# An eighth, half-deep set of block products for columns of the gate and the merge gate, an attention stage advanced at each half tile, and eleven warm-up matmuls

## The chip, the cores and the metric

The kernel runs on one core of one Trainium2 chip. The metric is the device time of one execution in microseconds (us), as the median of several runs.

Five engines work side by side and are tied by semaphores: TensorE (PE in the profile; its weight loads are listed apart as PEld), VectorE (DVE), ScalarE (ACT), GpSimd (POOL) and SyncE (SP). SP and POOL also hold the queues from which most DMA transfers are issued. Matmuls write their sums to PSUM, which the kernel uses as two rings of four banks, called `mm` and `bg`.

## What is computed

One decoder layer over 256 tokens and 2048 channels, in float32. A single input projection feeds two parallel token mixers and two merge gates:

```python
h = rmsnorm(x, pre_norm_g[l])
proj = h @ w_in[l]
(a_q, a_k, a_v, a_g, a_lr, b_q, b_k, b_v, b_g, m_a, m_b) = jnp.split(proj, offsets, axis=-1)
...
o_a = rmsnorm(o_a, gla_norm_g[l]).reshape(B, S, GLA_VAL_DIM) * jax.nn.silu(a_g)
y_a = o_a @ w_branch_a[l]
...
o_b = o_b.reshape(B, S, DIFF_VAL_DIM) * jax.nn.silu(b_g)
y_b = o_b @ w_branch_b[l]
merged = jax.nn.sigmoid(m_a) * y_a + jax.nn.sigmoid(m_b) * y_b
out = merged @ w_out[l]
x = x + rmsnorm(out, post_norm_g[l])
```

`o_a` is gated linear attention with 4 heads, `o_b` is differential attention with 16 heads. The change concerns 512 columns of `a_g` (the fourth group of the gate, "ag3" in the kernel) and 512 columns of `m_a` (the third group of the merge gate, "m02").

## The kernel before

**Three matmuls for one.** Each float32 operand is split into a part `hi` in a shorter format and the remainder `lo`. A product is the sum hi x hi, hi x lo and lo x hi. For the weights the split is made on the fly in half tiles of 128 x 1024: ACT writes `hi` (L345), DVE writes `lo` = raw - hi (L346). Both have rings of three buffers. `take` hands the next split half tile to the matmuls and emits the splits of up to three later half tiles (`AHEAD = 3`), in an order fixed beforehand in `seq`.

**Plain tiles.** `token_major` computes 512 columns for all 256 tokens over the full depth of 2048: eight half tiles, each of two depth blocks x two token halves x three matmuls = 12 matmuls of 512 columns. `channel_major` computes 128 channels with the channels on the partitions: two half tiles of 8 matmuls of 512 and 8 of 256 columns each.

**Sets of block products.** A set covers 1024 columns as two groups of 512, left and right, and forms the 2 x 2 block product (two token halves, two depth halves, two column groups) with seven products instead of eight, numbered 1 to 7 and run in the order `PRODUCTS = (1, 3, 5, 6, 2, 7, 4)`. The sums of token halves are made once, at the start. The sums of weight blocks are made while the set runs, in the tiles `a` and `b` of the tag `chain`, which has four slots: `link` loads a block, `follow_set` adds another block into it by a DMA with addition on POOL's queue (L240) or adds two tiles on DVE (L248), always after the split that reads the older value. Product 1 reads `a`; product 3 reads `b`; products 5, 6 and 4 read `a` after one more addition each; product 2 reads a third tile, `c`, that SP loads; product 7 reads `b` after one addition. There are seven sets, 0 to 6. Each product of a set has four half tiles (two quarters of the depth `t`, two halves `h` each) of 6 matmuls. The results of a set are combined in `block_products` and spilled to DRAM (`gspill`), from where later stages fetch them.

**The order of the phase.** `phase_steps` writes the order of the sets' half tiles by hand, with the half tiles of 88 other projections (`v4`, the keys and queries of both mixers) between them: one other half tile after each pair of half tiles of a set, two at the front, none at the places in `skip`. In this phase the matmuls are pinned to this order.

**After the phase** come ag0 to ag3 (the gate), m02, the heads of group 3 (eight channel projections dq30 to dk33), m03, then the branch projections y00 to y03, and a branch stage in which the half tiles of y03, y10 and y11 alternate with a smaller set `ys0`. Between their half tiles the attention runs as generators in a list `tasks`: `pump(n)` lets the first n tasks take one step each, after every second half tile of a plain tile and after each channel projection. `gla_scores` makes the scores of the linear attention in two halves, `gla_out` weighs the values (`weigh`, L513 in the profile) and transposes the result (`turn_heads`, L1016), and two lanes `diff_lane` run the pairs of heads of the differential attention. A task that yields "go" is called eager: `pump_eager` also lets it take a step after the half tiles in between. `settle` and the loop on `"out"` pump without matmuls of their own where a result is needed that is not there yet.

**The start.** `WARM` matmuls on ones run on TensorE before the first weights are split (L432). The first weights are those of v0, whose matmuls stand at L528.

Of the kernel before, what the change touches and what calls it, by code (L numbers as in the profile page):

```python
# [24 lines left out]
LANES = 3  # L25
X_LOADS = {0: (2, 2), 1: (4, 4), 2: (8, 4), 3: (12, 4)}
ROWS = {"two": 2, "tok": 4, "chan": KT}
WARM = 9
PRODUCTS = (1, 3, 5, 6, 2, 7, 4)
SETS = 7  # L30
MERGE = (0, 1, 6)
LEAD = 6
# [16 lines left out]
def chunk_plan():  # L49

    plan = [("v0", "two", "w_in", [(6144, RANK), (2048, 2 * VG[0] - RANK)])]
    at = 2 * VG[0] - RANK
    for g, n in enumerate(VG[2:]):
        plan.append((f"v{g + 2}", "tok", "w_in", [(2048 + at, n)]))
        at += n
    for hf in range(2):
        for name, base in (("k", 1024), ("q", 0)):
            for c in range(4):
                plan.append((f"{name}{hf}{c}", "chan", "w_in", [(base + 512 * hf + P * c, P)]))
    o = 6144 + RANK  # L60
    for s in range(2):
        plan.append((f"set{s}", "set", "w_in", [(o + 10240 + 1024 * s, 1024)]))
    for s in range(2, 6):
        plan.append((f"set{s}", "set", "w_in", [(o + base + 512 * (s - 2), 512) for base in (4096, 6144)]))
    plan.append(("set6", "set", "w_in", [(o + 8192, 1024)]))
    for g in range(4):
        plan.append((f"ag{g}", "tok", "w_in", [(4096 + 512 * g, 512)]))
        for c in range(4):
            for n, name in enumerate(("dq", "dk")):
                plan.append((f"{name}{g}{c}", "chan", "w_in", [(o + 2048 * n + 512 * g + P * c, P)]))  # L70
        if g > 1:
            plan.append((f"m0{g}", "tok", "w_in", [(o + 8192 + 512 * g, 512)]))
        for br in range(2):
            kind = "late" if br and g < 2 else "tok"
            plan.append((f"y{br}{g}", kind, ("w_branch_a", "w_branch_b")[br], [(512 * g, 512)]))
        plan.append((f"o{g}", "late", "w_out", [(512 * g, 512)]))
    plan.append(("ys0", "half", "w_branch_b", [(c, 512) for c in BRANCH_COLS]))
    for s, cols in enumerate(LATE_COLS):
        plan.append((f"os{s}", "half", "w_out", [(c, 512) for c in cols]))
    return plan  # L80


def tiles_of(n, kind):

    if kind == "set":
        return [(8 * i + 4 * t, 4, 512 * j, 512) for i in range(2) for j in range(2) for t in range(2)]
    if kind == "half":
        return [(4 * i, 4, 512 * j, 512) for i in range(2) for j in range(2)]
    if kind == "late":
        return [(r, 4, 0, n) for r in (8, 12)]  # L90
    return [(r, ROWS[kind], 0, n) for r in range(0, KT, ROWS[kind])]


def phase_steps():
# [4 lines left out]
    slots = [(s, prod, t) for s in range(SETS) for prod in PRODUCTS for t in range(2)]  # L99
    front = [(0, prod, t) for prod in PRODUCTS[:2] for t in range(2)]  # L100
    skip = [(SETS - 1, 4, 1)] + [(s, prod, 0) for prod in (4, 2, 1) for s in range(SETS - 1, 0, -1)]
# [35 lines left out]
def hybrid_kernel(ctx: ExitStack, tc, xt, xn, preg, postg, w, w2, gkb, glag, lamv, diffg, ident_d, causal_d, lmask_d, out):  # L137
# [75 lines left out]

    def link(s, name, t):
        count[0] += 1
        c = blocks.tile([P, 2048], F32, tag="chain", name=f"{name}_{count[0]}", bufs=4)
        (pool if s else sp).dma_start(c, weights(f"set{s}", {"a": 0, "b": 6}[name] + t)[0])
        chain[s, name, t] = c

    def emit_set(s, prod, t, h):  # L220
        c = slice(1024 * h, 1024 * h + 1024)
        if h == 0 and s + 1 < SETS and (prod, t) in ((7, 1), (4, 0)):
            link(s + 1, "a", 1 - t)
        if h == 0 and s + 1 < SETS and (prod, t) == (4, 1):
            link(s + 1, "b", 0)
        if h == 0 and prod == 1 and (s == 0 or t == 0):
            link(s, "b", t if s == 0 else 1)
        n = 4 * PRODUCTS.index(prod) + 2 * t + h + LEAD - 4 * PRODUCTS.index(2)
        if 0 <= n < 4:
            i, j = n // 2, n % 2  # L230
            raws[s, i, j] = u([P, 1024], "c")
            sp.dma_start(raws[s, i, j], weights(f"set{s}", 4 + i)[0][:, 1024 * j : 1024 * j + 1024])
# [3 lines left out]
    def follow_set(s, prod, t, h):  # L236
        c = slice(1024 * h, 1024 * h + 1024)

        def accumulate(name, i):
            pool.dma_start(chain[s, name, i][:, c], weights(f"set{s}", 2 + i)[0][:, c], accum_op=ALU.add)  # L240
# [3 lines left out]
        i = {(5, 1): 0, (6, 0): 1, (2, 1): 0, (7, 0): 1}.get((prod, t))  # L244
# [309 lines left out]
    def token_major(key, n, ops, step=1, upto=KT // 2):  # L554
        banks = [ps("mm"), ps("mm")]
        for q in range(upto):
            half_tile(banks, n, q, ops, *take(key))
# [188 lines left out]
    gspill = [None] * (2 * SETS)  # L746

    def merge_gate(banks):
        t = u2([P, 2, 512], "mgate")
        for b in range(2):  # L750
            act.activation(t[:, b, :], banks[b], AF.Tanh, scale=half_rstd[:, b : b + 1])
# [59 lines left out]
    def block_products(s):  # L811
# [4 lines left out]
        def right_done(b):  # L816
            dst = halves["r"][:, b, :]
            if s in MERGE:
# [6 lines left out]
        def left_done(b, src):  # L825
            if s in MERGE:
                act.activation(halves["l"][:, b, :], src, AF.Tanh, scale=half_rstd[:, b : b + 1])
            else:
                act.activation(halves["l"][:, b, :], src, AF.Copy, scale=rstd[:, b : b + 1])

        for prod in PRODUCTS:
# [3 lines left out]
            for t in range(2):  # L835
                for h in range(2):
                    hi, lo = take(("set", s, prod, t, h))
                    for w, parts in ((hi, (0, 1)), (lo, (0,))):
                        for j in range(2):
                            kt = 4 * t + 2 * h + j  # L840
                            a = operand(prod, kt)
                            for part in parts:
                                first = prod not in (6, 7, 4) and kt == 0 and w is hi and part == 0
                                last = kt == 7 and w is lo
                                i = mm(out, a[part], w[:, 512 * j : 512 * j + 512], start=first, stop=last, skip_group_check=out is x)
                    latest[0] = i.ins
                    if t and h:
# [25 lines left out]
    sets = (step for s in range(SETS) for step in block_products(s))  # L873
# [3 lines left out]
    for n, step in enumerate(phase_steps()):  # L877
        if n == PUT_OFF:
            put_off.pop()()
        if step == ("set", SETS - 1, 7, 1, 1):  # L880
# [103 lines left out]
    def gla_out():  # L984
# [44 lines left out]
        for n in range(6):  # L1029
# [6 lines left out]
            if n > 1:  # L1036
                for j in range(2):
                    turn_heads(n // 2 - 1, 2 * (n % 2) + j)
            yield
# [204 lines left out]

    for g in range(4):
        banks = token_major(f"ag{g}", 512, x_ops, LANES)
        t = u2([P, 2, 512], "ua")
        for b in range(2):
            gate(banks[b], b, t[:, b, :])
# [21 lines left out]
    merge_gate(token_major("m02", 512, x_ops, LANES))  # L1271
# [361 lines left out]
```

## Time and profile before

| What | Value |
|---|---|
| Median of 3 runs | 1090.25 us |
| Lowest and highest run | 1090.04 and 1090.7 us |
| The profiled execution | 1092.18 us |
| Its span in the trace | 1090.3 us |
| Instructions | 15340 |
| Phase of the sets, end | 590.65 us |
| ag0 to ag3, end | 689.2 us |
| m02, end | 717.6 us |
| Heads of group 3, end | 775.4 us |
| DMA moved | 285.06 MB, mean 261 GB/s |

The span is what the trace covers, from the first instruction to the last; the profiled execution's time has 1.9 us around it. The ends of the stages are read from the order of TensorE's matmuls in the chain of waits. In a row of grouped instructions stand line, engine, operation, tiles, shapes and count, then busy time and mean duration in ns, then the idle time before them with what ended it. In a row of a timeline stand start, duration, engine, line, operation and count. Busy times of TensorE are modelled from the issue of the matmuls.

### The profile page before, as it was taken

Reading aid. Unit: us, or ns where it says so; the run is one execution under the profiler, and the core shown is the slowest. Engines: PE = TensorE matmul, PEld = TensorE weight load, DVE = VectorE, ACT = ScalarE, POOL = GpSimd, SP = SyncE. Lnnn points to the kernel's source line nnn. Section 1 sums busy time; section 2 is a strip of 40 time slices with the busy share of each in tenths; the row PEclk is TensorE's granted clock in tenths of the full one; section 3 lists DMA queues with packets and bytes.
Section 4 is the critical chain, followed back from the end, with each engine's and each line's share of the span. In section 5 each row is a group of like instructions: output and inputs, shape, how many; then the busy total and the mean of one; then the engine's idle time right before and its main releaser. Section 6 shows DMA issues by size and latency. Waiting matters only on the chain.

```text
span 1090.3 us, 15340 instructions
## 1 busy us (share of the span) xinstructions
PE 1082.4 (99%) x5451; PEld 929.4 (85%) x5451; DVE 916.2 (84%) x1277; ACT 711.2 (65%) x1038; POOL 146.4 (13%) x217
## 2 busy tenths in 40 slices
PE   9999999999999999999999999999999999999997
PEld 8999888888888888888888888889888888888886
DVE  7787987978979989889798999658779867889886
ACT  6986766666666766667665655556777765566662
POOL 0201111121021121211221100020111011100000
PEclk9999999999999999999999999999999999999999
DMA  9889969789798797997986654597988869979752
GB/s 338 286 288 325 265 232 319 182 274 298 248 331 223 277 303 192 337 258 261 300 228 228 255 177 171 176 333 253 284 279 271 277 238 315 350 255 270 270 183 107
DMA packets 63757, 285.06 MB, mean 261 GB/s; under 512 B 8320, under 2 KB 11392, under 8 KB 45504
## 3 DMA queue, kind: packets, MB, share of 16 engines
q1 hardware_dynamic: 39808, 186.87, 48.7%
q0 software_dynamic: 23296, 96.48, 32.6%
q8 instruction: 43, 0.70, 0.3%
q10 hardware_dynamic: 576, 0.73, 0.2%
q14 instruction: 34, 0.28, 0.1%
HBM read 258.88 MB, written 25.17 MB: 261 GB/s over the span
## 4 chain that ended last, share of the span: by engine, by line
PE 93%; DMA 3%; DVE 2%; issue 1%; ACT 1%; POOL 0%; POOLq 0%; SPq 0%; ACTq 0%; DVEq 0%
PE mm L540 57%; PE bg L540 26%; DMA raw<-in_w_dram 3%; PE mm L528 2%; PE bg L528 2%; PE mm L513 1%; DVE lo L346 1%; PE bg L956 1%; PE bg L513 1%; ACT hi L345 0%; PE bg L1121 0%; PE bg L1095 0%; PE bg L1096 0%; PE bg L1133 0%; PE bg L1134 0%
## 5 line engine op out<-in xcount | busy, mean ns | idle before, releaser
L345 ACT ACTIVATE hi<-raw 128x1024 fp32r<-128x1024 f32 (+3 forms) x261 | 268.4, 1032 | 209.1 <-PE bg L540 102.5
L346 DVE TENSOR_TENSOR lo<-raw,hi 128x1024 fp32r<-128x1024 f32 (+3 forms) x263 | 310.5, 1185 | 91.3 <-ACT hi L345 87.9
L540 PE MATMUL mm<-hi,xs 128*128 128x512 f32 (+1 forms) x848 | 214.1, 386 | 0.0
L540 PEld LDWEIGHTS mm<-hi,xs 128*128 128x128 f32 x848 | 156.9, 188 | 25.9
L540 PE MATMUL bg<-xs,hi 128*128 128x512 f32 x640 | 164.8, 389 | 0.0
L346 DVE TENSOR_TENSOR lo<-a,hi 128x1024 fp32r<-128x1024 f32 x112 | 135.0, 1219 | 11.7 <-ACT hi L345 10.5
L540 PEld LDWEIGHTS bg<-xs,hi 128*128 128x128 f32 x640 | 120.3, 188 | 23.4
L345 ACT ACTIVATE hi<-a 128x1024 fp32r<-128x1024 f32 x112 | 118.6, 1060 | 30.8 <-PE mm L540 22.8
L540 PE MATMUL mm<-lo,xs 128*128 128x512 f32 (+1 forms) x424 | 117.7, 383 | 0.0
L540 PEld LDWEIGHTS bg<-xs,lo 128*128 128x128 f32 x640 | 87.3, 190 | 6.2
L540 PEld LDWEIGHTS mm<-lo,xs 128*128 128x128 f32 x424 | 79.4, 188 | 14.5
L540 PE MATMUL bg<-xs,lo 128*128 128x256 f32 x640 | 89.2, 282 | 0.0
L346 DVE TENSOR_TENSOR lo<-b,hi 128x1024 fp32r<-128x1024 f32 x56 | 67.4, 1221 | 7.8 <-ACT hi L345 6.8
L345 ACT ACTIVATE hi<-b 128x1024 fp32r<-128x1024 f32 x56 | 59.3, 1061 | 18.1 <-PE mm L540 15.5
L540 PE MATMUL mm<-hi,oah 128*128 128x512 f32 x128 | 50.8, 397 | 0.0
L540 PE MATMUL mm<-hi,oal 128*128 128x512 f32 x128 | 50.0, 391 | 0.0
L1107 ACT ACTIVATE prob<-prob,mx,score_scale 128x128 f32<-128x128 f32 x64 | 34.2, 536 | 10.7 <-DVE mx L1102 10.6
L240 POOL DMA_DIRECT2D b<-in_w_dram x28 | 24.4, 873 | 107.3 <-DVE a L248 103.4
L540 PE MATMUL mm<-hi,obh 128*128 128x512 f32 x96 | 37.7, 392 | 0.0
L540 PE MATMUL mm<-hi,obl 128*128 128x512 f32 x96 | 37.4, 390 | 0.0
L345 ACT ACTIVATE hi<-c 128x1024 fp32r<-128x1024 f32 x28 | 29.6, 1060 | 10.2 <-PE mm L540 5.4
L248 DVE TENSOR_TENSOR a<-a,b 128x1024 f32<-128x1024 f32 x28 | 34.1, 1221 | 0.4
(409 smaller groups left out, 2021.1 us busy)
## 6 DMA issues: line engine op xcount, KB each, us to landing
raw<-in_w_dram SPq DMA_DIRECT2D x114, 1024.0 KB, 6.3
a<-in_w_dram POOLq DMA_DIRECT2D x28, 512.0 KB, 13.9
c<-in_w_dram SPq DMA_DIRECT2D x28, 512.0 KB, 8.7
b<-in_w_dram POOLq DMA_DIRECT2D x28, 512.0 KB, 7.9
a<-in_w_dram POOLq DMA_DIRECT2D x12, 1024.0 KB, 5.3
b<-in_w_dram POOLq DMA_DIRECT2D x12, 1024.0 KB, 8.8
raw<-in_w_dram SPq DMA_DIRECT2D x14, 832.0 KB, 6.5
dh<-dh POOLq DMA_DIRECT2D x16, 256.0 KB, 4.4
```

What stands on the lines that cost most here:

```text
L240: pool.dma_start(chain[s, name, i][:, c], weights(f"set{s}", 2 + i)[0][:, c], accum_op=ALU.add)
L248: dve.tensor_tensor(out=a, in0=a, in1=chain[s, "b", i][:, c] if second else raws[s, i, h], op=ALU.add)
L345: act.activation(hi_t[:, a:b], r[:, a:b], AF.Copy)
L346: dve.tensor_tensor(out=lo_t[:, a:b], in0=r[:, a:b], in1=f32(hi_t[:, a:b]), op=ALU.subtract)
L513: i = pe.matmul(out, lhs, rhs, start=first and n == 0, stop=last and n == len(pairs) - 1, **kw)
L528: i = pe.matmul(banks[g][b][:, :n], a[part][:, P * b : P * b + P], w[:, n * g : n * g + n], start=first, stop=last)
L540: i = pe.matmul(*args, **kw)
L956: pe.matmul(o, xk[:, P * c : P * c + P], xq.rearrange("p (b c t) -> p b c t", b=2, c=4)[:, :, c, :], start=i == 0, stop=i == 1)
L1107: act.activation(prob[m][:, lo:up], prob[m][:, lo:up], AF.Exp, scale=score_scale[:, b : b + 1], bias=mx[:, i : i + 1], accum_out=z[:, i : ...
```

## The change

An eighth set, number 7, is added for the columns of ag3 (left) and m02 (right), but over half of the depth only: the first quarter and the third, four blocks of 128 each. Each of its seven products has two half tiles instead of four. Its results are spilled without an activation. The plain tiles of ag3 and m02 keep the other half of the depth (kind `rest`, four half tiles each); at their end DVE adds the fetched part of the set to the gate, and subtracts the fetched part from the merge gate's banks. The skip list of the phase grows from 14 to 21 places, since the number of other projections stays. `gla_out` starts its transposes one step later, runs seven steps instead of six, and yields "go". `WARM` goes from 9 to 11.

```diff
...
 ROWS = {"two": 2, "tok": 4, "chan": KT}
-WARM = 9
+WARM = 11
 PRODUCTS = (1, 3, 5, 6, 2, 7, 4)
 SETS = 7
+QUARTER = ("ag3", "m02")
 MERGE = (0, 1, 6)
...
     plan.append(("set6", "set", "w_in", [(o + 8192, 1024)]))
+    plan.append((f"set{SETS}", "quarter", "w_in", [(5632, 512), (o + 9216, 512)]))
     for g in range(4):
-        plan.append((f"ag{g}", "tok", "w_in", [(4096 + 512 * g, 512)]))
+        plan.append((f"ag{g}", "rest" if g == 3 else "tok", "w_in", [(4096 + 512 * g, 512)]))
         for c in range(4):
...
         if g > 1:
-            plan.append((f"m0{g}", "tok", "w_in", [(o + 8192 + 512 * g, 512)]))
+            plan.append((f"m0{g}", "rest" if g == 2 else "tok", "w_in", [(o + 8192 + 512 * g, 512)]))
         for br in range(2):
...
         return [(8 * i + 4 * t, 4, 512 * j, 512) for i in range(2) for j in range(2) for t in range(2)]
+    if kind == "quarter":
+        return [(8 * i, 4, 512 * j, 512) for i in range(2) for j in range(2)]
+    if kind == "rest":
+        return [(r, 4, 0, n) for r in (4, 12)]
     if kind == "half":
...
     slots = [(s, prod, t) for s in range(SETS) for prod in PRODUCTS for t in range(2)]
+    slots += [(SETS, prod, 0) for prod in PRODUCTS]
     front = [(0, prod, t) for prod in PRODUCTS[:2] for t in range(2)]
-    skip = [(SETS - 1, 4, 1)] + [(s, prod, 0) for prod in (4, 2, 1) for s in range(SETS - 1, 0, -1)]
+    skip = [(SETS, 4, 0), (SETS - 1, 4, 1), (SETS - 2, 4, 1)] + [(s, prod, 0) for prod in (4, 2, 1) for s in range(SETS - 1, 0, -1)]
     skip = skip[: len(slots) + len(front) - len(other)]
...
+    def block(s, i, t):
+        return weights(f"set{s}", i if s == SETS else 2 * i + t)[0]
+
     def link(s, name, t):
...
         c = blocks.tile([P, 2048], F32, tag="chain", name=f"{name}_{count[0]}", bufs=4)
-        (pool if s else sp).dma_start(c, weights(f"set{s}", {"a": 0, "b": 6}[name] + t)[0])
+        (pool if s else sp).dma_start(c, block(s, {"a": 0, "b": 3}[name], t))
         chain[s, name, t] = c
...
         c = slice(1024 * h, 1024 * h + 1024)
-        if h == 0 and s + 1 < SETS and (prod, t) in ((7, 1), (4, 0)):
+        few = 1 if s == SETS else 2
+        if h == 0 and s < SETS and (prod, t) in ((7, 1), (4, 0)) and (t or s + 1 < SETS):
             link(s + 1, "a", 1 - t)
-        if h == 0 and s + 1 < SETS and (prod, t) == (4, 1):
+        if h == 0 and s < SETS and (prod, t) == (4, 1):
             link(s + 1, "b", 0)
-        if h == 0 and prod == 1 and (s == 0 or t == 0):
+        if h == 0 and prod == 1 and s < SETS and (s == 0 or t == 0):
             link(s, "b", t if s == 0 else 1)
-        n = 4 * PRODUCTS.index(prod) + 2 * t + h + LEAD - 4 * PRODUCTS.index(2)
-        if 0 <= n < 4:
+        n = 2 * few * (PRODUCTS.index(prod) - PRODUCTS.index(2)) + 2 * t + h + LEAD
+        if 0 <= n < 2 * few:
             i, j = n // 2, n % 2
             raws[s, i, j] = u([P, 1024], "c")
-            sp.dma_start(raws[s, i, j], weights(f"set{s}", 4 + i)[0][:, 1024 * j : 1024 * j + 1024])
+            sp.dma_start(raws[s, i, j], block(s, 2, i)[:, 1024 * j : 1024 * j + 1024])
         a, b = chain[s, "a", t], chain[s, "b", t]
...
         def accumulate(name, i):
-            pool.dma_start(chain[s, name, i][:, c], weights(f"set{s}", 2 + i)[0][:, c], accum_op=ALU.add)
+            pool.dma_start(chain[s, name, i][:, c], block(s, 1, i)[:, c], accum_op=ALU.add)
...
             accumulate("a", t)
-        i = {(5, 1): 0, (6, 0): 1, (2, 1): 0, (7, 0): 1}.get((prod, t))
+        steps = {(5, 0): 0, (2, 0): 0} if s == SETS else {(5, 1): 0, (6, 0): 1, (2, 1): 0, (7, 0): 1}
+        i = steps.get((prod, t))
         if i is not None:
...
         banks = [ps("mm"), ps("mm")]
-        for q in range(upto):
-            half_tile(banks, n, q, ops, *take(key))
+        for q in (2, 3, 6, 7) if key in QUARTER else range(upto):
+            half_tile(banks, n, q, ops, *take(key), begin=4 if key in QUARTER else 0)
             if q % 2 or not ts:
...
-    gspill = [None] * (2 * SETS)
-
-    def merge_gate(banks):
+    gspill = [None] * (2 * SETS + 2)
+
+    def merge_gate(banks, parts=None):
         t = u2([P, 2, 512], "mgate")
         for b in range(2):
-            act.activation(t[:, b, :], banks[b], AF.Tanh, scale=half_rstd[:, b : b + 1])
+            src = banks[b]
+            if parts:
+                src = parts[b]
+                dve.tensor_tensor(out=src, in0=banks[b], in1=src, op=ALU.subtract)
+            act.activation(t[:, b, :], src, AF.Tanh, scale=half_rstd[:, b : b + 1])
         m0.append(spill(t, "mgate"))
...
             dst = halves["r"][:, b, :]
+            if s == SETS:
+                return
             if s in MERGE:
...
                 act.activation(halves["l"][:, b, :], src, AF.Tanh, scale=half_rstd[:, b : b + 1])
-            else:
+            elif s < SETS:
                 act.activation(halves["l"][:, b, :], src, AF.Copy, scale=rstd[:, b : b + 1])
+            elif b:
+                act.activation(halves["l"][:, b, :], src, AF.Copy)
...
             out = bank[prod]
-            for t in range(2):
+            few = 1 if s == SETS else 2
+            for t in range(few):
                 for h in range(2):
...
                                 first = prod not in (6, 7, 4) and kt == 0 and w is hi and part == 0
-                                last = kt == 7 and w is lo
+                                last = kt == 4 * few - 1 and w is lo
                                 i = mm(out, a[part], w[:, 512 * j : 512 * j + 512], start=first, stop=last, skip_group_check=out is x)
                     latest[0] = i.ins
-                    if t and h:
+                    if t == few - 1 and h:
                         if prod in (1, 5):
...
-    sets = (step for s in range(SETS) for step in block_products(s))
+    sets = (step for s in range(SETS + 1) for step in block_products(s))
     rest = others()
...
             put_off.pop()()
-        if step == ("set", SETS - 1, 7, 1, 1):
+        if step == ("set", SETS, 7, 0, 1):
             fetched = [[fetch(ts[name, hf], name, u) for name in ("q", "k")] for hf in range(2)]
...
             yield
-        for n in range(6):
+        for n in range(7):
             if n < 4:
...
                 done.add("weighed")
-            if n > 1:
+            if n > 2:
                 for j in range(2):
-                    turn_heads(n // 2 - 1, 2 * (n % 2) + j)
-            yield
+                    turn_heads((n - 3) // 2, 2 * ((n - 3) % 2) + j)
+            yield "go"
         done.add("out")
...
+    def other_parts(n):
+        return [fetch(gspill[n][:, b, :], "rest", lambda shape, name, dtype: t2(shape, name)) for b in range(2)]
+
     for g in range(4):
+        parts = other_parts(2 * SETS) if g == 3 else None
         banks = token_major(f"ag{g}", 512, x_ops, LANES)
...
         for b in range(2):
-            gate(banks[b], b, t[:, b, :])
+            src = banks[b]
+            if parts:
+                src = parts[b]
+                dve.tensor_tensor(out=src, in0=banks[b], in1=src, op=ALU.add)
+            gate(src, b, t[:, b, :])
         gates.append(t)
...
     m0.extend(gspill[12:14])
-    merge_gate(token_major("m02", 512, x_ops, LANES))
+    parts = other_parts(2 * SETS + 1)
+    merge_gate(token_major("m02", 512, x_ops, LANES), parts)
     diff_heads(3)
...
```

## Prediction

> **What bounds the kernel now.** The page's first part, the engines' busy times, comes first: is one engine full? Then the chain of waits, to see whether that engine also sets the end. Then what TensorE itself waited for.
>
> ```profile
> PE 1082.4 (99%) x5451; PEld 929.4 (85%) x5451; DVE 916.2 (84%) x1277; ACT 711.2 (65%) x1038; POOL 146.4 (13%) x217
> PE 93%; DMA 3%; DVE 2%; issue 1%; ACT 1%; POOL 0%; POOLq 0%; SPq 0%; ACTq 0%; DVEq 0%
> PE bg L432 <- DVE ones_b L429: 1.6, 1, 1.6
> PE bg L1571 <- ACT diag L1570: 1.0, 1, 1.0
> PE mm L528 <- ACT hi L342: 0.5, 1, 0.5
> ```
>
> A busy PE alone proves little, because its ends are modelled. The wait rows are stronger: apart from the start and the last transpose product, TensorE is never recorded as waiting. So a matmul saved is time saved, and a new wait of TensorE costs its full length. Third come the stages around the change, busy time per window: the last set, ag0, a stretch of ag1, and the heads of group 3.
>
> ```profile
> 510.60:590.65 80.05, 80.05 (x399) 68.03 (x398) 70.47 (x75) 56.02 (x65) 15.82 (x24) 1.00 0.83 261
> 590.65:612.40 21.75, 21.75 (x97) 18.02 (x96) 18.61 (x24) 9.50 (x12) 4.06 (x6) 1.00 0.65 214
> 613.00:638.00 25.00, 25.00 (x125) 21.11 (x124) 24.97 (x35) 16.00 (x22) 2.65 (x5) 1.00 0.73 266
> 717.60:775.40 57.80, 57.80 (x355) 51.42 (x355) 42.16 (x106) 35.32 (x79) 9.52 (x16) 1.00 0.89 281
> ACT hi L345 <- PE mm L540: 138.8, 166, 2.7
> ```
>
> Behind the window and its length stand the busy times of PE, PEld, DVE, ACT and POOL, the clock, and the share of DMA. DVE is at 70.47/80.05 = 88% in the set stage, full in the stretch of ag1, at 73% in the heads. The last row shows the cover: ACT's splits stand waiting for TensorE to free a buffer, so they run as far ahead as three buffers allow.
>
> **TensorE's work.** One set of two half tiles and one plain stretch of two half tiles, each 24 matmuls of 512 columns, and a channel projection, 32 matmuls:
>
> ```profile
> 230.14 5.47 PE mm L540 x24
> 689.24 5.46 PE mm L540 x24
> 717.82 5.57 PE mm L540 x32
> ```
>
> A matmul of 512 columns costs 5.46/24 = 0.2275 us, a set's half tile (6) 1.365, a plain half tile (12) 2.73, half a projection 2.78. Removed: ag3 and m02 lose half their depth, 8 of 16 half tiles, 96 matmuls, 21.84 us. Added: seven products of two half tiles, 84 matmuls, 19.11 us. Net **-2.73 us**, all of it on the path.
>
> **The warm-up.**
>
> ```profile
> 1.59 4.02 PE L432 MATMUL bg<-ones_b 128*128 128x512 bf16 x9 [1.59 <-DVE ones_b L429]
> 6.15 1.72 PE L528 MATMUL mm<-hi,xs 128*128 128x416 f32 x4 [0.54 <-ACT hi L342]
> 7.67 1.59 PE L528 MATMUL bg<-hi,xs 128*128 128x416 f32 x4
> 9.75 0.59 PE L528 MATMUL bg<-lo,xs 128*128 128x416 f32 x2
> 10.18 0.92 PE L528 MATMUL mm<-hi,xs 128*128 128x416 f32 x4
> 10.94 0.92 PE L528 MATMUL bg<-hi,xs 128*128 128x416 f32 x4
> ```
>
> From 6.15 to 9.75 ten real matmuls take 0.36 us each, from 10.18 on four take 0.76, 0.19 each. The slow stretch begins after a 0.54 us hole between the ninth warm-up and the first operand. Two more, at 4.02/9 = 0.45 us, close the hole and overrun it by 0.36. Ends: a loss of 0.4, if the slow stretch stays; a gain of 10 x 0.17 = 1.7, if it vanishes because the hole caused it and the overrun is only the modelled end of a matmul. I take **-1.0**, nearer the second: the stretch starts at the hole, and the nine warm-ups before it lasted longer (4.02) than the stretch did (3.6). The Trainium skill, "TensorE: Matmul & The Clock Gate", section "Part 1: The HAM clock gate", says that the full clock is granted after one busy window of about 3.4 us, that windows run free of the kernel, and that the count of cold matmuls changes from run to run. By that rule, with the hole closed, the slow stretch would end between 5.0 and 8.4, an estimate from the page's window, and this term would be -0.7 to -1.7; by the same rule it would differ from run to run. The trace agrees in the 3.6, and one trace can't show the rest.
>
> **What else the new set issues.** Durations:
>
> ```profile
> L346 DVE TENSOR_TENSOR lo<-a,hi 128x1024 fp32r<-128x1024 f32 x112 | 135.0, 1219 | 11.7 <-ACT hi L345 10.5
> L345 ACT ACTIVATE hi<-a 128x1024 fp32r<-128x1024 f32 x112 | 118.6, 1060 | 30.8 <-PE mm L540 22.8 <-PE bg L540 5.5 <-DMA a<-in_w_dram 0.8
> L248 DVE TENSOR_TENSOR a<-a,b 128x1024 f32<-128x1024 f32 x28 | 34.1, 1221 | 0.4
> L853 DVE TENSOR_TENSOR p<-mm,p 128x512 f32<-128x512 f32 x7 | 4.8, 683 | 0.0
> L756 DVE TENSOR_TENSOR dq<-bg,dq 128x256 f32<-128x256 f32 x12 | 5.0, 418 | 0.0
> ```
>
> DVE: 14 splits and 4 additions at 1.22, four merges at 0.68: 24.7 us. The skip list, longer by seven, leaves six projection halves in this set, each some 1.65 (split, head sums at 0.42, their spill). So 34.6 us of DVE stand beside 19.1 + 6 x 2.78 = 35.8 of TensorE, 97%. It fits, on the lead that the splits have; ends 0 and 1 us, I take 0.2. The eight fewer plain splits, the two additions of 0.68 at the end of ag3 and of m02, and ACT's six more splits at 1.06 lie in stages with room. Bytes: 5 MB for the set, less 4, plus 1 MB of spill and 1 of fetch, where DMA stands at 0.65 to 0.89: nothing.
>
> **The accumulate, first new wait.** Product 1 reads block a, then POOL's queue adds another block into it by DMA, and product 5 reads it again. With two half tiles per product the distance shrinks to four set halves and two projection halves, 4 x 1.365 + 2 x 2.78 = 11.0 us from TensorE's start on product 1. (SP's block loads and the links of a and b on POOL's queue move with the set; they wait only for slots that set 6 gives up after its products 7.)
>
> ```profile
> 527.36 1.07 PE L540 MATMUL mm<-hi,xs 128*128 128x512 f32 x4
> 527.43 0.86 POOL L240 DMA_DIRECT2D a<-in_w_dram  x1 [1.79 <-DVE lo L346]
> a<-in_w_dram POOLq DMA_DIRECT2D x28, 512.0 KB, 13.9
> b<-in_w_dram POOLq DMA_DIRECT2D x28, 512.0 KB, 7.9
> DMA to landing us min/median/max: 5.6/11.1/18.9
> ```
>
> The issue comes 0.07 after TensorE's start; the split needs 1.06 and about 0.25 of signalling. So TensorE waits from a landing of 11.0 - 1.4 = 9.6 us on. Into b it takes 7.9, into a 13.9; but today's into a come behind two links of 1 MB each on the same queue, and the new set links one, earlier. I take 8 to 9.5 and **+0.3** (0, and 1.9 at 11.5). ACT stands in line behind that split, and DVE behind ACT, so the lower split, 1.22 against the 4 x 0.2275 = 0.91 of matmuls that cover it, adds 0.3 for each of the two half tiles, 0.6.
>
> **Attention, two more.** Pumps are counted from the code: ag3 and m02 give two each instead of four, so weighing starts at the third projection of group 3, and the lanes have four pumps fewer before the branch. One weighing step, the fetch that follows it, and its landings:
>
> ```profile
> 708.28 2.06 PE bg L513 x9
> 712.65 0.54 POOL L176 DMA_DIRECT2D vback<-vl  x1
> vback<-vl POOLq DMA_DIRECT2D x1, 512.0 KB, 4.3
> vback<-vl POOLq DMA_DIRECT2D x1, 512.0 KB, 7.4
> ```
>
> The fetch for the step after next is issued 4.4 us after a step starts, and lands at 8.7 to 11.8. At each half tile that next-but-one step comes after 2 x (2.06 + 2.78) = 9.7, its second matmul at 9.9. So 0 to 1.9 of wait, **+0.6**. Its transposes stay two half tiles behind the weighing, as they stood one pump of two half tiles behind it: nothing.
>
> The lanes' last pairs: weighted sums of TensorE, then their result on DVE, then the transposes that wait for it.
>
> ```profile
> 881.67 0.22 PE bg L1134 x2
> 884.64 0.61 DVE L1145 SCALAR_TENSOR_TENSOR ogb<-bg,de,ub 128x128 f32<-128x128 f32 x2
> 887.70 0.44 PE mm L1151 x4
> ```
>
> From 881.89 to 885.25 is 3.4 us; today 5.8 lie between. By the count the last two pairs fall at the branch, where steps are one half tile apart: 2.73 + 0.33 for the one, 2.73 for the other. That is 0.4 + 0.8 with signalling: **+1.2** (0 if those transposes are issued later in TensorE's order; 2.5 if a split of 1.2 gets in between). Behind the waiting transpose stands every matmul.
>
> **Sum**: -2.73 - 1.0 + 0.2 + 0.3 + 0.6 + 1.2 = -1.4, with 0.3 taken off for waits that overlap (a delay of TensorE lets the later fetch land): **-1.7**. The profiled execution took 1092.18 us, its span 1090.3 and 1.9 around it; it would become 1090.5. It stands 1.9 above the median of the runs, 1090.25, which becomes **1088.5**.
>
> **Rivals.**
> *The waits stay hidden.* Landings at 4.3 and below 9.6, the transposes put later: -2.73 with 0 to -1.7 of the warm-up, 1085.8 to 1087.5, about 1086.7. For it: splits are ahead everywhere, and TensorE shows no wait in 1070 us of such steps. Against it: 2.73 is less than 3.4.
> *The warm-up doesn't do what it is for.* The slow stretch falls on the real matmuls again: +0.4 in place of -1.0, with my waits 1090.0. For it speaks that nine warm-ups of 4.02 us didn't bring the full clock either.
> *Slower: the accumulate lands late.* At 14, as the rows into a have it, TensorE waits 4.4 and DVE's refill adds 0.6; -3.7 + 5.0 + 1.8 = +3.1, 1093.3. It decides from a landing of about 13 on. Against it: one link, not two, and that well ahead.
>
> **How the numbers follow.** A measurement of this kernel can tell about 0.2% from no change, 2.2 us. My forecast 0.42; waits hidden 0.36; no gain from the warm-up 0.10; late accumulate 0.12. Faster by over 0.2% takes nearly all of the second: 0.36. Slower takes 0.10 of the last and 0.01 of the third: 0.11. The rest, 0.53, lies within. The range goes from everything gained and nothing paid (-4.4, 1085.9) to the late accumulate in its milder half, 1092.2.
>
> **What would show it.** TensorE's waits: a row at L540 behind hi in the new set (the accumulate), at L513 behind vback, at the turned-out transposes behind ogb near the branch. At the start: 0.19 instead of 0.36 us a matmul right after the warm-ups. The set stage longer by 19.1 us, ag3 and m02 together shorter by 21.8. Wrong would be a wait that I don't name: in ag1, where DVE is fullest, or in the links between sets 5 and 6, now eight set halves in a row.

## The result, and the profile after

| | before | after |
|---|---|---|
| Median | 1090.09 us (1089.42 to 1090.7, 6 runs) | 1097.7 us (1096.68 to 1099.41, 6 runs) |
| Ratio | | 1.0071, 95% interval 1.0058 to 1.0084 |
| Profiled execution, its span | 1092.18 us, 1090.3 us | 1098.33 us, 1096.5 us |

The change made the kernel 7.6 us slower. The forecast was 1.7 us faster, and the time lies above the whole range.

First the engines' busy times and the chain of waits, from the page of the kernel after.

```profile
PE 1081.7 (99%) x5441; PEld 927.8 (85%) x5441; DVE 931.6 (85%) x1295; ACT 721.3 (66%) x1047; POOL 154.2 (14%) x229
...
PE 93%; issue 3%; DMA 2%; DVE 1%; POOL 1%; ACT 0%; SPq 0%; POOLq 0%; ACTq 0%
```

These rows hardly differ from those before, and show why a page of shares is not enough here: 7.6 us are 0.7% of the span. What TensorE waited for tells more (us in total, times, longest).

```profile
PE bg L525 <- DMA vback<-vh: 3.8, 1, 3.8
PE mm L1172 <- DVE ogb L1166: 2.1, 1, 2.1
...
PE bg L525 <- DMA vback<-vl: 1.3, 1, 1.3
```

These three rows are new (the only other new row is one of 0.2), at two of the places where the prediction put a wait: the weighing product (line 513 before, 525 now) behind the fetched `vback`, and the turned-out transposes (1151 before, 1172 now) behind `ogb`. The third place, the accumulate in the new set, has no row.

**The first place.** TensorE's timeline around the third weighing (start, duration, what; in brackets the idle time before it and what ended it):

```profile
734.99 0.39 PE L552 MATMUL mm<-xs,hi 128*128 128x512 f32 x1
739.14 0.56 PE L525 MATMUL bg<-vback,ath 128*128 128x512 f32 x1 [3.76 <-DMA vback<-vh]
741.05 0.79 PE L525 MATMUL bg<-vback,ath 128*128 128x512 f32 x1 [1.35 <-DMA vback<-vl]
...
744.63 2.73 PE L552 MATMUL mm<-xs,hi 128*128 128x512 f32 x8
...
748.15 0.63 PE L525 MATMUL bg<-vback,ath 128*128 128x512 f32 x2
```

Eight matmuls of a projection stand with 2.73 us here, and with 1.98 in undisturbed stretches of this kernel. The windows say why (the seventh figure, behind the busy times of five engines, is the granted clock of TensorE, the next the share of DMA):

```profile
735.40:739.10 3.70, 0.00 (x0) 0.00 (x0) 2.68 (x5) 1.33 (x2) 1.17 (x3) 1.00 1.34 260
739.60:746.40 6.80, 5.45 (x14) 4.24 (x14) 0.16 (x1) 1.89 (x5) 0.44 (x1) 0.51 1.13 284
```

The reader is to see two losses in one: TensorE stands for 5.1 us, and for 6.8 us after that the clock is 0.51. The rows of waits show only the first. And the landings of the two pairs that are fetched during the weighings (from two windows of the DMA view; the last figure is us from issue to landing), with the lane's placement of `kh` that was issued among them:

```profile
vback<-vh POOLq DMA_DIRECT2D x1, 512.0 KB, 9.4
vback<-vl POOLq DMA_DIRECT2D x1, 512.0 KB, 10.8
kh<-dh SPq DMA_DIRECT2D x1, 128.0 KB, 9.3
...
vback<-vh POOLq DMA_DIRECT2D x1, 512.0 KB, 9.2
vback<-vl POOLq DMA_DIRECT2D x1, 512.0 KB, 10.9
```

The prediction took 4.3 and 7.4 for the same fetches from the kernel before.

**The second place**, the first of the last two lane pairs at the branch, on four engines:

```profile
903.45 1.05 ACT L357 ACTIVATE hi<-raw 128x1024 fp32r<-128x1024 f32 x1
904.40 0.26 ACT L1159 ACTIVATE junkd<-bg 128x128 bf16<-128x128 f32 x1
...
904.70 1.22 DVE L358 TENSOR_TENSOR lo<-raw,hi 128x1024 fp32r<-128x1024 f32 x1
...
906.99 0.61 DVE L1166 SCALAR_TENSOR_TENSOR ogb<-bg,de,ub 128x128 f32<-128x128 f32 x2
...
906.07 0.69 POOL L459 TENSOR_TENSOR de<-de,neg_half 128x2 f32<-128x2 f32 x1 [6.94 <-DVE de L1162]
...
904.94 0.38 PE L1172 MATMUL mm<-ident,ogb 128*128 128x128 f32 x2
907.39 0.59 PE L1172 MATMUL mm<-ident,ogb 128*128 128x128 f32 x2 [2.07 <-DVE ogb L1166]
```

The chain from the weighted sums to `ogb` runs over four engines, and both of the weight splits, 1.05 on ACT and 1.22 on DVE, got in between. That is the case from which the prediction made the upper end of this term, 2.5.

### The profile page after: what moved, and what is told of

It is laid out like the page before. It is cut to its first block, busy times and chain, and to the rows that moved or that the text cites. A ratio compares the mean times of both kernels' runs of the same rounds, so it can differ in the third digit from the quotient of the medians.

```text
span 1096.5 us, 15366 instructions
## 1 busy us (share of the span) xinstructions
PE 1081.7 (99%) x5441; PEld 927.8 (85%) x5441; DVE 931.6 (85%) x1295; ACT 721.3 (66%) x1047; POOL 154.2 (14%) x229
## 4 chain that ended last, share of the span: by engine, by line
PE 93%; issue 3%; DMA 2%; DVE 1%; POOL 1%; ACT 0%; SPq 0%; POOLq 0%; ACTq 0%
PE mm L552 57%; PE bg L552 27%; PE mm L540 2%; PE bg L540 2%; PE mm L525 1%; DMA vback<-vl 1%; PE bg L977 1%; DMA part_e<-in_w_dram 1%; PE bg L525 1%; PE bg L444 0%; PE bg L1142 0%; PE bg L1116 0%; PE bg L1343 0%; PE bg L1037 0%; DVE lo L358 0%
## 5 line engine op out<-in xcount | busy, mean ns | idle before, releaser
L357 ACT ACTIVATE hi<-raw 128x1024 fp32r<-128x1024 f32 (+3 forms) x253 | 259.3, 1031 | 185.8 <-PE bg L552 92.3
L358 DVE TENSOR_TENSOR lo<-raw,hi 128x1024 fp32r<-128x1024 f32 (+3 forms) x255 | 300.8, 1184 | 61.7 <-ACT hi L357 58.8
L552 PE MATMUL mm<-hi,xs 128*128 128x512 f32 (+1 forms) x808 | 204.2, 385 | 0.0
L552 PEld LDWEIGHTS mm<-hi,xs 128*128 128x128 f32 x808 | 149.8, 188 | 24.8
L358 DVE TENSOR_TENSOR lo<-a,hi 128x1024 fp32r<-128x1024 f32 x120 | 144.7, 1220 | 22.1 <-ACT hi L357 21.3
L357 ACT ACTIVATE hi<-a 128x1024 fp32r<-128x1024 f32 x120 | 127.1, 1060 | 45.2 <-PE mm L552 28.5
L552 PE MATMUL mm<-lo,xs 128*128 128x512 f32 (+1 forms) x404 | 112.8, 383 | 0.0
L552 PEld LDWEIGHTS mm<-lo,xs 128*128 128x128 f32 x404 | 75.7, 188 | 13.6
L358 DVE TENSOR_TENSOR lo<-b,hi 128x1024 fp32r<-128x1024 f32 x60 | 72.4, 1221 | 6.5 <-ACT hi L357 5.0
L357 ACT ACTIVATE hi<-b 128x1024 fp32r<-128x1024 f32 x60 | 63.4, 1061 | 16.6 <-PE mm L552 14.6
```

Source lines behind the costliest of these rows:

```text
L357: act.activation(hi_t[:, a:b], r[:, a:b], AF.Copy)
L358: dve.tensor_tensor(out=lo_t[:, a:b], in0=r[:, a:b], in1=f32(hi_t[:, a:b]), op=ALU.subtract)
L552: i = pe.matmul(*args, **kw)
```

## The experiments

Each ratio is to the kernel before, run on the same chip; its median was 1090.1 to 1090.2 us there. c2 is one execution beside one of the kernel before, 1091.96 us. a4, b1 and c1 have four executions each, a1 five, the others ten or eleven.

| Run | us (median, range) | ratio, 95% interval |
|---|---|---|
| a1, stages of attention's output undone | 1094.2 (1093.37 to 1094.73) | 1.0032, 1.0019 to 1.0045 |
| a2, both late pairs fetched early | 1091.76 (1090.74 to 1094.03) | 1.0016, 1.0006 to 1.0025 |
| c1, first lane one step later | 1100.18 (1099.8 to 1101.36) | 1.0092, 1.0077 to 1.0107 |
| a4, the kernel before with the stages alone | 1099.2 (1097.08 to 1101.9) | 1.0075, 1.0057 to 1.0092 |
| a3, the kernel before with 11 warm-ups alone | 1090.28 (1089.48 to 1090.88) | 0.9996, 0.9987 to 1.0005 |
| b1, more steps in the shortened tiles | 1098.91 (1095.87 to 1101.69) | 1.0076, 1.0057 to 1.0095 |
| b2, a2 and b1 together | 1089.73 (1088.65 to 1090.42) | 0.9992, 0.9983 to 1.0001 |
| b3, a1 and b1 together | 1092.43 (1088.88 to 1094.93) | 1.0014, 0.9999 to 1.0028 |
| b4, a1, a2 and b1 together | 1088.1 (1087.58 to 1089.65) | 0.9978, 0.9969 to 0.9987 |
| d1, b4 with nine warm-ups | 1087.87 (1087.42 to 1089.58) | 0.9978, 0.9969 to 0.9987 |
| c2, both lanes behind the weighings | 1098.83 (one run) | |

### Is the wait for vback the loss, and what makes the fetch late?

a1 puts the stages back to one in two half tiles:

```diff
-        for n in range(7):
+        for n in range(6):
...
-            if n > 2:
+            if n > 1:
                 for j in range(2):
-                    turn_heads((n - 3) // 2, 2 * ((n - 3) % 2) + j)
-            yield "go"
+                    turn_heads(n // 2 - 1, 2 * (n % 2) + j)
+            yield
```

> The changed kernel with attention's output put back to a stage every second half tile (six stages), set 7 and 11 warm-up matmuls kept. Theory F (fetch): about 8.2 of the us lost by the change are the third weighing's wait for the vback pair of TensorE line 525, and the slower clock after it; with the old stages the fetch has twice the time, so the wait and the clock dip go and the time falls by about 8.2 to some 1089.5 (1088.5 to 1091), with the late lane pairs at the branch still costing 2 to 4. Rival S (spread): the time lost is not in that wait alone but in shorter half tiles and late lanes all along; then the time stays above 1094.

a2 keeps the stages and brings all pairs early:

```diff
-        while "scores1" not in done or len(gates) < 4:
+        while len(gates) < 4:
+            yield
+        bring(2)
+        bring(3)
+        while "scores1" not in done:
             yield
...
-            if n < 2:
-                bring(n + 2)
```

> The changed kernel with the stages at each half tile kept, but the third and fourth vback pairs fetched as soon as gate 3 is there, ahead of the first weighing, instead of behind the first and second weighing. Theory F: the wait at line 525 goes entirely, 1097.7 - 8.2 = 1089.5 (1088.5 to 1091). Rival C (cadence): the weighings at each half tile stall TensorE themselves, over banks, ScalarE or VectorE, and the fetch is only the last to be named; then another wait takes its place and the time stays above 1094.

Neither has a row for `vback`, and in a2 no other wait took its place at the weighings, so rival C falls. What the wait cost comes out of a2 almost by itself, because its first two weighings start where those of the kernel after do (725.44 and 730.37, against 725.46 and 730.38 us). Its timeline at the third and the fourth:

```profile
735.21 0.62 PE L525 MATMUL bg<-vback,ath 128*128 128x512 f32 x2
...
737.27 1.98 PE L552 MATMUL mm<-xs,hi 128*128 128x512 f32 x8
...
740.03 0.63 PE L525 MATMUL bg<-vback,ath 128*128 128x512 f32 x2
```

The fourth weighing starts at 740.03 rather than 748.15: the late pair cost **8.1 us**. The two profiled executions are only 1098.33 - 1091.4 = 6.9 apart, since a2 lost more at the branch. There the wait is the old one, 1.9 us at the transposes of the lanes, and behind it the clock falls, as it didn't in the profiled execution of the kernel after:

```profile
899.30:902.70 3.40, 3.40 (x14) 3.15 (x14) 2.17 (x5) 1.81 (x6) 0.44 (x1) 0.51 0.93 375
902.80:907.00 4.20, 4.20 (x23) 3.51 (x22) 2.61 (x8) 2.57 (x6) 1.45 (x4) 1.00 1.01 393
```

3.4 us at 0.51 are 1.7 us lost, nearly as much as the wait itself. So a2 missed my 1089.5 by a price that I had left out. a1 missed it by more: undoing the stages puts the second lane, which starts behind the fourth weighing, one step of the pump later, and the last pairs deeper into the branch. TensorE's waits in a1:

```profile
PE mm L1172 <- DVE ogb L1166: 3.2, 2, 2.9
...
PE bg L1153 <- ACT prob L1144: 0.8, 1, 0.8
```

That is 4.0 us of waiting, and 3.4 us at clock 0.51 on top (behind a wait of 2.85). By its number a1 lies where rival S put it, above 1094; but most of what it lost stands in these two rows and the slow stretch, at the branch, and not all along. So the new stages are not only harm: they bring the lanes forward by a step.

Then the cause of the late landing. a4 is the kernel before with the stages alone (the reverse of a1's edit), c1 the kernel after with one edit in the first lane:

```diff
         last = None
+        if n == 0:
+            yield
         ask()
```

> The kernel before with nothing but the stages of attention's output at each half tile. Theory F, with P or D: the same wait for vback appears without set 7, and the time is 1090.1 + 4 to 8 = 1094 to 1098, with no wait at the branch, since the lanes end two steps earlier there. Rival Q (the quarter tiles): the collision of fetches and placements comes from the pump steps that set 7 moved; then there is no wait at line 513 here and the time is 1089.5 to 1090.5.

> The changed kernel with the first lane's start put off by one step of the pump (one added yield), so that its four kh placements on SP's queue come some 5 us later, and the fetches of vback are where they were. Theory P (placements): the vback pair landed 9.4 and 10.8 us after issue, rather than 3.5 to 7.4 as before, because the kh placements moved at the same time; so here it lands in 4 to 7.5, the wait of 3.8 at line 525 falls to 0 to 2 and the time to 1089 to 1092 (the lane pairs come one step later at the branch, plus or minus 1). Rival D (deadline): two half tiles are too few for the fetch whatever runs beside it; then the landing stays over 9 and the time at 1097 plus or minus 1.5.

In a4 the wait is there without set 7, quarter tiles or warm-ups, and larger (waits of TensorE):

```profile
PE bg L513 <- DMA vback<-vl: 5.1, 2, 2.7
...
PE bg L513 <- DMA vback<-vh: 1.0, 1, 1.0
PE mm L1151 <- DVE ogb L1145: 0.8, 1, 0.8
```

So the stages at each half tile make the loss, and set 7 is not needed for it: rival Q falls. The time, 1099.2, lies above my 1094 to 1098. c1 gave the landings that theory P wanted, for one pair. The DMA view of c1 at the issue of the first of the two pairs, and of the second, which one of the lane's placements shares:

```profile
vback<-vh POOLq DMA_DIRECT2D x1, 512.0 KB, 3.6
vback<-vl POOLq DMA_DIRECT2D x1, 512.0 KB, 4.2
...
vback<-vh POOLq DMA_DIRECT2D x1, 512.0 KB, 6.6
vback<-vl POOLq DMA_DIRECT2D x1, 512.0 KB, 8.7
...
q<-dh SPq DMA_DIRECT2D x1, 128.0 KB, 7.3
```

The first pair is issued at 730.63 and 731.21, and the first placement now behind it, at 733.85. So the first pair lands in 3.6 and 4.2 instead of 9.4 and 10.8, and the third weighing waits for nothing. The placements then meet the second pair, and the fourth weighing waits 0.9 and 2.1. (The profile names VectorE for the 0.9, which ended its work for this product at 742.09; `vh` landed at 735.40 + 6.6 = 742.0, and the product starts at 742.11. Either may have been the last.) The time did not fall, because the collision had moved rather than gone, and because the lanes ended later (3.2 at `ogb`, as in a1, with a second stretch at half clock). My 1089 to 1092 was wrong.

c2 was to take the placements away from both pairs:

```diff
-        while ("scores1", "weighed")[n] not in done:
+        while "weighed" not in done:
```

> The changed kernel, stages at each half tile and the late fetches kept, with both lanes started only behind the fourth weighing, so that no kh placement stands on SP's queue while the vback pairs are fetched. The time is no matter here (the lanes end later, and the branch pays for it, 1097 to 1104). Theory P (placements): both pairs land in 3.5 to 7.4 us, as in the kernel before, and TensorE's waits at line 525 come to under 1 us together. Rival D (deadline): with the steps 4.8 us apart the third or the fourth weighing waits 1.5 us or more all the same.

The DMA view of c2 where the second pair is issued:

```profile
vback<-vh POOLq DMA_DIRECT2D x1, 512.0 KB, 7.3
vback<-vl POOLq DMA_DIRECT2D x1, 512.0 KB, 8.7
q<-dl SPq DMA_DIRECT2D x2, 128.0 KB, 6.1
```

It did so for the first pair only, which landed in 3.5 and 4.2 us. SP's queue runs ahead of TensorE: the placements of `q` were issued from 733.28 on, 9 us before the fourth weighing started. So they were again in flight with the second pair (7.3 and 8.7), and the fourth weighing waited 1.6 and 1.4 us (the profile names VectorE for the 1.6, but `vh` landed at 734.75 + 7.3 = 742.05, just before the product started at 742.23).

One more transfer has to be looked at: a weight load of 1 MB on SP's queue was in flight beside each slow pair of the kernel after, c1 and c2 for part of the time. In the kernel after it was issued at 723.91 and landed at 733.1. In a4 the load before had landed at 712.0, ahead of the first pair, and the next was issued at 717.54. The load in the kernel after, and `vh` of the first pair in a4:

```profile
raw<-in_w_dram SPq DMA_DIRECT2D x1, 1024.0 KB, 9.2
```

```profile
vback<-vh POOLq DMA_DIRECT2D x1, 512.0 KB, 5.4
```

In the kernel after, `vh` for the third weighing, issued at 729.65, shared 3.4 us with the load and then took 5.9 more, beside the placements and with the next pair behind it in its queue; alone a whole fetch took 3.6. In a4 `vh` landed in 5.4 with `kh` beside it, at 717.6, as the next load was only being issued; in the kernel before, with `kh` behind it, it landed in 3.5. So the placements make the fetch late without a weight load; what the load adds where both are in flight was not separated.

Neither P nor D is right alone. A fetch with nothing beside it lands 4.2 us after its issue, in time for a weighing that starts 5.0 us after it (735.21 - 730.23), and beside the placements, `q` or `kh`, it landed in 5.4 to 12.0 (the 12.0 is the second pair of a4), too late for these stages in most cases. Whether the placements hold it back by their bytes or by their number of packets wasn't tried.

### Is the branch paid for by the steps that the short tiles leave out?

b1 adds a step after each of the four half tiles of `ag3` and `m02`; b2 is this edit with a2's, b3 with a1's.

```diff
-            if q % 2 or not ts:
+            if q % 2 or not ts or key in QUARTER:
```

> The changed kernel with a step of the pump after each of the four half tiles of gate 3 and of merge gate 2 (four each, as many as before, rather than two). Theory T (steps lost): the wait of 2.1 us for ogb at the branch and the half clock after it come from the four steps that the shortened tiles don't take; so here the last lane pair is out before the branch as in the kernel before, that row vanishes, and 2.5 to 4 us go; the wait for vback stays (8 us), so 1093.5 to 1095.5. Rival V (VectorE and GpSimd are behind anyway, by set 7's added work): the row at the branch stays and the time is 1097 or more.

> The two edits together on the changed kernel: the third and fourth vback pairs fetched ahead of the first weighing, and a step after each half tile of the shortened tiles. Theories F and T: both waits go and nothing takes their place; from 1091.8 of the first edit alone, 1.9 of wait, 0.3 beside it and 1.7 for 3.4 us at half clock go: 1087.5 to 1088.2, faster than before. Rival V: the wait at the branch stays and the time is 1091 or more.

> The changed kernel with attention's output back at six stages, one each step of the pump, and a step after each half tile of the shortened tiles: set 7 and the warm-up, with neither the early weighings nor the lost steps. Theories F and T: no wait for vback and none at the branch, 1087.5 to 1088.2. Where steps lie one half tile apart in merge gate 2, weighings may still come 2.7 us apart: then a part of the wait for vback comes back and the time is 1089 to 1092.

TensorE's waits in b1:

```profile
PE bg L525 <- DMA vback<-vh: 4.5, 1, 4.5
PE bg L525 <- DMA vback<-vl: 2.0, 1, 2.0
...
PE mm L1172 <- DVE ogb L1166: 0.8, 1, 0.8
```

The wait at the branch is gone; the 0.8 that is left lies at 782 us, at an early pair, as in a4. Theory T holds. The time did not fall: the executions of b1 lie around those of the kernel after, and the profiled one has a longer stall at the weighing (6.4 of waiting and again 6.8 us at half clock). My 1093.5 to 1095.5, which took that stall as fixed, was wrong. b2 has neither wait, and only the 0.8 and a 0.2. It came out at 1089.7, against my 1087.5 to 1088.2; the two waits are 1.0 of that, and I did not place the rest. b3, at 1092.4, lies above both of my ranges and spread over 6 us: five of its ten executions took 1088.9 to 1091.3, five 1093.6 to 1094.9. The profile, of one at 1088.88, shows 1.0 of waiting at `vback` and no fall of the clock behind it. The mean granted clock of the whole execution is 0.996 to 0.997 in three of the five that took longer and 0.998 in the other two, and 0.998 to 0.999 in the first five, so those three probably lost clock; where they waited is not known, since none of them was profiled.

### What the two warm-up matmuls bring

a3 changes the number alone, in the kernel before, and d1 takes it back in the best version.

> The kernel before with 11 warm-up matmuls instead of nine and nothing else. Theory W (the hole): closing the 0.54 us hole gives the full clock to the first real matmuls in every execution; phase 2 starts 2.0 us earlier, and the time is 1090.2 - 2.0 = 1088.2 (1087.6 to 1088.7). Rival G (the moment is not the kernel's): the profiled execution of before stood at 1092.2, 2 us above the median of its own runs, so it was one of the few in which the clock came late; then most executions of before have nothing to gain, the median stays at 1089.6 to 1090.4, and only the executions at 1092 vanish.

The profile of a3 shows what the prediction hoped for, full speed from the first real matmul, 1.00 us for four instead of 1.72:

```profile
6.05 1.00 PE L528 MATMUL mm<-hi,xs 128*128 128x416 f32 x4
6.88 0.92 PE L528 MATMUL bg<-hi,xs 128*128 128x416 f32 x4
```

Yet the median is that of the kernel before. Of the 27 executions of before run with it, seven took 1091.26 to 1092.57 us, and twenty 1089.3 to 1090.64; a3's eleven lie at 1089.48 to 1090.88. The profiled execution, at 1092.18, is like the seven, and that the slow stretch which I priced is what makes these seven longer is likely, but no other of them was profiled. Rival G holds for the median. Its other half, that the executions at 1092 vanish, fits a3, which has none; but with 7 such in 27, eleven executions would have none in 4% of cases by chance, (20/27) to the eleventh power.

b4 joins the edits of a1, a2 and b1, and is the version without any of the new waits; d1 is b4 with `WARM = 9`.

> Set 7 and 11 warm-up matmuls with all that was found: six stages of attention's output as before the change, the third and fourth vback pairs fetched ahead of the first weighing, and a step of the pump after each half tile of the shortened tiles. Theory F with T: no wait of TensorE over 0.5 us but the one at the end that every kernel here has; in no execution the half clock that took 3 to 5 us in half the executions of the kernel without the early fetch; the arithmetic of the matmuls is what is left: 1090.2 - 2.7 = 1087.5 (1086.9 to 1088.3), and a spread under 2 us. Rival: the early fetch takes slots or DMA from something else, as in the kernel with seven stages (0.8 at ogb, 0.2 at part): then 1088.5 to 1090.

> The kernel with all three edits, but with nine warm-up matmuls as before the change. Theory G (the clock comes at a moment of its own): most executions equal those with 11, and about a quarter are 2 us longer, as 7 of 27 of the kernel before were; the median differs by less than 0.6. Theory W (the hole decides): all are longer by 1.7 to 2.0.

TensorE's waits in b4, and the start of d1 on TensorE's timeline:

```profile
PE bg L444 <- DVE ones_b L441: 1.6, 1, 1.6
PE bg L1603 <- ACT diag L1602: 1.0, 1, 1.0
PE mm L540 <- ACT hi L354: 0.5, 1, 0.5
PE bg L552 <- DVE lo L358: 0.4, 1, 0.4
```

```profile
1.59 3.50 PE L444 MATMUL bg<-ones_b 128*128 128x512 bf16 x9 [1.59 <-DVE ones_b L441]
6.06 0.99 PE L540 MATMUL mm<-hi,xs 128*128 128x416 f32 x4 [0.96 <-ACT hi L354]
```

With nine warm-ups, and a hole of 0.96 us behind them that is larger than the 0.54 of the profile before, the first real matmuls ran at full speed: a hole alone does not make them slow. Nor does an execution that takes longer always have a slow start: b4's profiled one, with 11 warm-ups, is its slowest at 1089.65, and its first four real matmuls took 0.99 us, as in d1. b4 and d1 beat both kernels, at the same ratio, 0.9978; b4 came into my 1086.9 to 1088.3, and d1's median within the 0.6 of theory G. The matmul arithmetic is left: -2.73 forecast, 1087.87 - 1090.11 = -2.2 and 1088.1 - 1090.11 = -2.0 measured. Set 7 is worth nearly its matmuls, if the other edits in b4 and d1 only take away waits; the kernel before shows none that they could have taken away. No other part of the change showed a gain of its own in the median.

## Why the prediction was wrong

The step that failed is the term for the fetch: +0.6 was taken, and 8.1 measured. All terms, in order:

**TensorE's work, -2.73: right.** The same group of matmuls at the end of `ag0` stands at 611.34 in a3 and at 630.10 in the kernel after, which began 0.24 earlier: 18.8 + 0.2 = 19.0 for the new set, 19.1 forecast.

```profile
611.34 2.00 PE L540 MATMUL mm<-hi,xs 128*128 128x512 f32 x8
```

```profile
630.10 2.00 PE L552 MATMUL mm<-hi,xs 128*128 128x512 f32 x8
```

**VectorE +0.2, accumulate +0.3: not there.** TensorE waited for neither in the set stage, and the 19.0 leaves no room for them. In the kernel after, the two accumulates into `a` of set 7 landed 5.6 and 7.8 us after their issue, where 8 to 9.5 was taken and 9.6 could be borne. The slower rival, a late accumulate, got the sign of the total right and the place wrong.

**Warm-up, -1.0: wrong for the median.** The step that failed is the base. I subtracted a saving seen in the profiled execution from the median of the runs, after noting that the one stood 1.9 us above the other. Those 1.9 us were the saving: the ten matmuls at 0.36 instead of 0.19 that I counted, 1.7 us, are what set that execution apart: at the end of `ag0` its group of matmuls stands at 613.10, 1.8 behind the 611.34 of a3. The Trainium skill, "TensorE: Matmul & The Clock Gate", section "Part 1: The HAM clock gate", says that the windows run free of the kernel and the count of cold matmuls changes from run to run. The times of the runs fit that: 7 of 27 were longer. I cited it, and drew a size from it rather than a frequency.

**The fetch for the third weighing, +0.6 (0 to 1.9): 8.1.** The mechanism was right, and its place; the term was mis-sized, in two parts. The issues came 4.2 and 4.8 us after the step's start (4.4 taken), and the need 9.8 after it (9.7 taken). The landing was taken from the kernel before, 4.3 to 7.4, where the lane's placements of `kh` start 2.7 us after the first pair's last issue. With stages at each half tile they start as the first pair is issued, and it landed at 9.4 and 10.8. I counted the instructions that the changed stages issue, and not those of the lane that had been moved to the same moment. The second part is the clock. The prediction says that "a new wait of TensorE costs its full length"; this one was 5.1 long and cost 8.1.

**The last lane pairs, +1.2 (0 to 2.5): right in kind, low in size.** 2.07 of waiting and 0.2 at the second pair in the profiled execution (its four transposes took 0.89 us, and 0.69 in a2), with the splits in between as my upper end had it; beyond the 2.5 where the clock falls too, as in a2 (1.9 + 1.7).

**Overlap, -0.3: wrong.** The waits were not softened by each other. In the profiled execution -2.73 + 8.1 + 2.07 + 0.2, and 0.2 for a wait at `ob_copy` that a3 has not, make 7.8; it stood 1098.33 - 1090.11 = 8.2 above that of a3, and the 0.4 between I did not place.

The range failed on the same term: its upper end, 1092.2, came from a late accumulate, and the bound of the fetch from one kernel's landings, which are no bound once the traffic beside them moves.

The Trainium skill, "TensorE: Matmul & The Clock Gate", section "HAM oscillation — how this bites in real kernels", warns of idle gaps of TensorE over about 3.4 us. The runs show a fall behind shorter ones: 1.9 us of waiting was followed by 3.4 us at half clock in a2, though 2.07 was not in the kernel after, nor 2.40 in a4. By the rule as it stands the second place would have cost its wait alone.

## What to carry to other kernels

When stages are pulled together, list every queue's transfers at the new moment, not only those of the code that was edited, and take a fetch's landing from a place with the same traffic beside it; then issue it as early as its buffers allow, which in b4 brought no new wait of TensorE. Before pricing something seen in one profiled execution, compare that execution's time with the median: if it is an outlier by just that amount, the saving is not in the median. On a kernel bound by TensorE, price a stall of about 2 us or more at its length and, as these runs have it, up to nearly as much again for the clock (nothing for 2.07 in the kernel after, 1.7 for 1.9 in a2, 3.0 for 5.1).

## What the hardware showed that I had not expected

The clock after a stall: the granted clock was 0.51 for 3.4 us after waits of 1.9 us (a2) and 2.85 us (a1), and for 6.8 us after 3.76 and 1.35 (the kernel after); it stayed full after 2.07 us in the kernel after and after 2.40 us in a4 (1.00 from 720.62 to 726.00). A stall of about the same length therefore had two prices in these executions. That is the likeliest reason for the 2.7 us between the fastest and the slowest execution of the kernel after: the mean granted clock is 0.996 in its three slower executions and 0.997 to 0.998 in its three faster ones, but only one of them was profiled.

A fetch of 512 KB over GpSimd's queue landed 3.5 to 4.2 us after issue alone (c1, c2) and 5.4 to 12.0 beside transfers of 128 KB on SyncE's queue (the kernel after, a4, c1, c2), with a weight load of 1 MB in flight for part of the time.
